# Trunk of retention, pooling, cross-attention and gated MLP: the value product's first weight splits are tied to the eleventh turned tile, and VectorE takes the pool groups' two carry copies from GpSimd

## The chip, the cores and the metric

The kernel runs on one core of one Trainium2 chip. The metric is device time in microseconds (us) of one launch, as the median of several runs. Beside the timed runs there is one profiled execution, whose trace gives start, length and waits of each instruction. All positions below are us from the start of that execution's span.

## The reference

One layer over a sequence of 2048 tokens with 1024 channels, all in f32. What matters here is the first half: a projection whose columns go to two mixers, an output projection with a residual, and a cross-attention into 256 memory tokens; a gated MLP and a last norm follow.

```
h = rmsnorm(x, mix_norm_g)
q, k, v, g, u = split(h @ w_in)
y_ret  = silu(g) * head_rmsnorm(retention(q, k, v))
# four channel groups of u, trailing windows 2, 4, 8, 16:
y_pool = ((window_sum(u) / count - u) @ pool_w) * pool_scale
x = x + concat(y_ret, y_pool) @ w_out
x = x + softmax(q' k'^T / 16) v' @ wo        # cross-attention, 4 heads
x = x + (silu(gate(c)) * val(c)) @ w_down    # c: causal conv of x_n @ w_up
out = rmsnorm(x, final_norm_g)
```

A trailing window of 16 tokens reaches back over the edge of a tile of tokens, so the kernel carries the last 16 columns of each group from one tile to the next.

## The kernel before, in words

Activations stand transposed: 128 channels on the partitions, tokens along the free dimension. The sequence is cut in two batches of 1024 tokens (`b` = 0, 1), each in two halves of 512 (`s`). Every f32 product is made of three TensorE passes (`passes`, L239): each operand is held as a rounded part and a rest, and high x high, high x low and low x high are added up in PSUM. So each weight tile and each activation tile that enters a product is first split: ScalarE writes the rounded part (L233, or L236 with a scale), and VectorE subtracts it from the source to get the rest (L234, which the profile books on the helper line L216, or L225 for the scaled form).

`unit` (L285) is one weight tile's work: `pairs` (L255) splits the tile's two halves into places of the tile Q, of which there are three; then 48 passes run, and an evacuation function is called per half of the tokens. `load_tile` (L303) fetches the tile into one of five places of R.

The stages of the first half, per batch: the value projection, four heads with their retention interleaved, the four pool groups in the order 0, 3, 2, 1 (in the second batch groups 3 and 2 come first of all, before the projection), the output projection (eight units whose contraction takes the groups' outputs last), the attention, and the value product (eight units, L1565 to L1580).

A pool group's evacuation (`pool_group`, L624) writes a half's 512 columns to a tile `u`, with 16 columns of room ahead of them. L630 copies the 16 carried columns `phalo` in there, L631 saves the last 16 columns of this half to `phalo` for the next. Then VectorE builds the window sum by doubling (additions over 527, 525, 521 and 513 columns, L636), takes the mean minus the token, and the result is split into the tile G. Both copies stand on GpSimd (the profile's POOL), in one queue with the DMAs that add up weight sums for the MLP (L915 to L922, four of them per job, each of which waits for an earlier one to land). POOL works its queue in order, as all engines do.

The attention (`attention`, L822) makes 16 score tiles (2 head pairs x 8 blocks of 128 tokens). For each: 24 passes, a row maximum on VectorE (L871), two exponentials on ScalarE (L875), the reciprocal (L877) and two scalings on VectorE, and `turn` (L847): four TensorE transposes (L850) and a split of the result. A tile is turned two tiles after its scores. The first tile needs the norm's factors, a chain of some 15 small VectorE operations (L267 to L272). In the second batch the MLP's first input tiles are normed beside it (`first_tiles`, L1453), on VectorE, GpSimd and the DMAs. The value product of the turned tiles follows; the last write of its weights VWd to DRAM is issued at 286.8 us, so for their fetch and split only room in R and Q and the engines' queues count.

The order of the instructions on each engine is set when the program is built, by a scheduler that plays the program through with its own durations; it places an instruction where its inputs are ready in that play. On the chip each engine then keeps that order.

Of the kernel before, what the change touches and what calls it, by code (L numbers as in the profile page):

```python
# [2 lines left out]

# [5 lines left out]
F32 = mybir.dt.float32  # L9
# [110 lines left out]
def trunk(ctx, tc, xT, memT, pos, w_qkgu, w_v, wkv, wqT, wo, wout_r, wout_p, poolT, w_up, w_dn, vecs, consts, outT):  # L120
# [94 lines left out]
    def tt(eng, out, a, b, op):  # L215
        return eng.tensor_tensor(out=out, in0=a, in1=b, op=op)  # L216
# [13 lines left out]
    def split(src, hi, lo, g=None):  # L230

        if g is None:
            act.activation(hi, src, AF.Copy)  # L233
            tt(dve, lo, src, hi.bitcast(F32), ALU.subtract)  # L234
        else:
            act.activation(hi, src, AF.Identity, scale=g)  # L236
            stt(lo, src, g, hi.bitcast(F32), ALU.mult, ALU.subtract)
# [17 lines left out]
    def pairs(raw):  # L255

        out = []
        for h in range(2):
            r = raw[h] if isinstance(raw, list) else raw[:, h * SUB : (h + 1) * SUB]
            pr = new_pair()  # L260
            split(r, pr[:, 0], pr[:, 1])
            out.append(pr)
        return out
# [13 lines left out]

    quarter, slow = [0], [True]
    behind, under, fetched = [iter(())], [iter(())], [None]

    def finish():
        for _ in behind[0]:
# [2 lines left out]
    def unit(raw, rhs, evac, order=range(4)):  # L285


        hs = pairs(raw)
        ps = [mmps() for _ in range(NS)]
        for h in range(2):  # L290
            for s in range(NS):
                for j, kk in enumerate(order):
                    k = 4 * h + kk
                    w = [hs[h][:, i, kk * P : (kk + 1) * P] for i in range(2)]
                    passes(ps[s], w, rhs(k, s), h + j == 0, h == 1 and j == 3)
                next(behind[0], None)
                quarter[0] += 1
                if not slow[0] or quarter[0] % 2:
                    next(under[0], None)
                if h == 1:  # L300
                    evac(s, ps[s])

    def load_tile(src, room=None):  # L303
        raw = new_raw() if room is None else room.f
        fetched[0] = sp.dma_start(raw, src.rearrange("p k n -> p (k n)"))
        return raw
# [317 lines left out]
    def pool_group(b, g, rb):  # L624
        out = B.take(2)

        def evac(s, ps):
            u, *bufs = [TT.take() for _ in range(3 if g else 2)]
            tt(dve, u.f[:, 16 : 16 + SUB], ps, rb[s].f[:, :SUB], ALU.mult)
            pool.tensor_copy(u.f[:, 0:16], phalo[:, g])  # L630
            pool.tensor_copy(phalo[:, g], u.f[:, SUB : SUB + 16])  # L631
            src, lo = u, 1
            for i in range(g + 1):
                sh = 1 << i
                dst = bufs[i % 2]
                tt(dve, dst.f[:, lo : 16 + SUB], src.f[:, lo : 16 + SUB], src.f[:, lo - sh : 16 + SUB - sh], ALU.add)  # L636
                src = dst
                lo += 2 * sh
            cur, d = u.f[:, 16 : 16 + SUB], src.f[:, 16 : 16 + SUB]
            w = 2 << g  # L640
            if b == 0 and s == 0:
                tt(dve, d[:, :w], d[:, :w], icnt[:, :w], ALU.mult)
                ts(dve, d[:, w:], d[:, w:], 1.0 / w, ALU.mult)
                tt(dve, d, d, cur, ALU.subtract)
            else:
                stt(d, d, 1.0 / w, cur, ALU.mult, ALU.subtract)
            split(d, out.r[:, s * SUB : (s + 1) * SUB], out.r[:, T + s * SUB : T + (s + 1) * SUB])
            for r in (u, *bufs):
                r.free()

        unit(load_tile(w_qkgu[12 + g]), xpair, evac)
        return out
# [152 lines left out]
    def add_residual(b, n, s_acc, got=None, acc=None):  # L805


        def evac(s, ps):
            cols = slice(s * SUB, (s + 1) * SUB)
            d = acc.f[:, cols] if got is None else got[s].f[:, :SUB]  # L810
            tt(dve, d, d, ps, ALU.add)
            if got is not None:
                split(d, *xpair(n, s))
                act.dma_start(Xd[b, n][:, cols], d)
            squares(n, d, s_acc[s].f[:, :SUB])
            if got is not None:
                got[s].free()

        return evac


    def attention(sums, beside, pace):  # L822


        scl, nscl = (smp.tile([P, 8], F32, tag="scl", name=nm("scl"), bufs=2) for _ in range(2))
        room = B.take(2 * KT)
        third = [Region(B, room.first + KT * i, KT) for i in range(2)] + [new_z(F32R).take(KT)]
        prob = [third[1], third[0]]

        def load_m(hp):  # L830

            out = mw[hp]
            for kp in range(KT // 2):
                raw = new_raw()
                fetched[0] = sp.dma_start(raw.rearrange("p (k n) -> p k n", k=2), Md[hp, 2 * kp : 2 * kp + 2].rearrange("k p n -> p k n"))
                if hp == 0 and kp == 0:

                    out += [(pr[:, 0], pr[:, 1]) for pr in pairs(raw)]
                    yield
                    continue  # L840
                for i in range(2):
                    u = third[2 * hp].r[:, (2 * kp + i) * T : (2 * kp + i + 1) * T]
                    split(raw[:, i * SUB : (i + 1) * SUB], u[:, :SUB], u[:, SUB:])
                    out.append((u[:, :SUB], u[:, SUB:]))
                yield

        def turn(pt, t, e):  # L847
            tp = aux()
            for j in range(4):
                pe.transpose(tp[:, j * P : (j + 1) * P], e.f[:, j * P : (j + 1) * P], ident)  # L850
            pt4 = pt.r.rearrange("p (i k t) -> p i k t", i=2, t=T)[:, :, :, t * P : (t + 1) * P]
            split(tp.rearrange("p (k t) -> p k t", k=4), pt4[:, 0], pt4[:, 1])
            e.free()

        mw = [[], []]
        for _ in load_m(0):
            pass
        more_m = load_m(1)
        late = []
        for i in range(2 * KT):  # L860
            hp, t = divmod(i, KT)
            ps = mmps()
            for k in range(KT):
                x2 = [X[:, 2 * k + j, t * P : (t + 1) * P] for j in range(2)]
                passes(ps, x2, mw[hp][k], k == 0, k == KT - 1)
            if i == 0:
                rn, _, _ = norm_tables(sums, wide=False)
                ts(dve, scl, rn, 1.0 / 16.0, ALU.mult)
                ts(dve, nscl, rn, -1.0 / 16.0, ALU.mult)
            mx, sm = small(2), small(2)  # L870
            dve.reduce_max(out=mx, in_=ps.rearrange("p (h m) -> p h m", h=2), axis=AX.X)  # L871
            ts(dve, mx, mx, nscl[:, t : t + 1], ALU.mult)
            e = TT.take()
            for j in range(2):
                act.activation(e.f[:, j * NMEM : (j + 1) * NMEM], ps[:, j * NMEM : (j + 1) * NMEM], AF.Exp,  # L875
                               bias=mx[:, j : j + 1], scale=scl[:, t : t + 1], accum_out=sm[:, j : j + 1])
            dve.reciprocal(sm, sm)  # L877
            for j in range(2):
                ej = e.f[:, j * NMEM : (j + 1) * NMEM]
                ts(dve, ej, ej, sm[:, j : j + 1], ALU.mult)  # L880
            if len(late) == 2:
                turn(*late.pop(0))
            late.append((prob[hp], t, e))
            for _ in range(pace):
                next(under[0], None)
            if i < KT - 2:
                next(more_m, None)
            else:
                for _ in range(pace):
                    next(beside, None)  # L890

        def end():
            for one in late:
                yield turn(*one)

        return prob, end()
# [599 lines left out]
    for b in range(NB):  # L1496
# [68 lines left out]
        for n in range(KT):  # L1565
            if n + 1 < KT:
                fetch_acc(n + 1)

            def rhs(k, s):
                at = (k % 4) * T + s * SUB  # L1570
                return tuple(prob[k // 4].r[:, i * 4 * T + at : i * 4 * T + at + SUB] for i in range(2))

            unit(load_tile(VWd[n]), rhs, add_residual(b, n, xs, acc=acc[n]))
            act.dma_start(Xd[b, n], acc[n].f)
            if b + 1 < NB:
                load_x(n, nxt, got)
                if n + 1 < KT:
                    got = fetch_x(b + 1, n + 1)
            elif n in (1, 3, 5):
                combine(rds[0], n // 2)  # L1580
# [143 lines left out]
```

## Time and profile before

| what | us |
|---|---|
| timed, three runs | 2504.08, 2498.81, 2500.07; median 2500.07 |
| profiled execution, its own time | 2497.77 |
| its span, first to last instruction | 2496.0 |
| TensorE busy (11390 passes) | 2439.3 (98%) |
| VectorE busy | 1699.9 (68%) |
| ScalarE busy | 1220.0 (49%) |
| GpSimd busy | 387.9 (16%) |

The profiled execution is 2.30 us below the median of the three runs. TensorE is busy nearly all the time, so the table alone shows that a change to the other engines can only act through the few stretches in which TensorE waits. In a timeline row, the number in brackets is how long the engine sat idle before the instruction, and the name behind the arrow is what ended that.

### The profile page before, as it was taken

How to read it: one execution, taken by the hardware profiler on the slowest of the kernel's cores; microseconds unless marked ns; L12 is line 12 of the kernel's file. 1: busy time of each engine (PE TensorE's matmuls, PEld its weight loads, DVE VectorE, ACT ScalarE, POOL GpSimd, SP SyncE). 2: the span in 40 equal slices, each digit the busy share in tenths (PEclk: the TensorE clock that was granted, in tenths of full speed). 3: DMA queues.
4: the chain of work that ended last, by engine and by line, in shares of the span. 5: the costliest groups of instructions: out<-in, count | busy, mean ns of one | idle time of the engine just before them, and what ended most of it. 6: DMA issues, size and time to landing. Idle time of an engine off the chain costs nothing. (4 is left out here: it accounts for less than half of the span.)

```text
span 2496.0 us, 33121 instructions
## 1 busy us (share of the span) xinstructions
PE 2439.3 (98%) x11390; PEld 2035.1 (82%) x11390; DVE 1699.9 (68%) x2757; ACT 1220.0 (49%) x2171; POOL 387.9 (16%) x396
## 2 busy tenths in 40 slices
PE   6999999999999999999998999999999999999997
PEld 6888887888788888888886888888888887888885
DVE  8646566564636574665777776896677687877875
ACT  6333423443321223424654555675555576666663
POOL 1010122100121110030025130332113021000001
PEclk9999999999999999999999999999999999999998
DMA  9363888716766664365567565665456468768951
GB/s 319 90 169 110 249 189 233 234 41 207 218 142 151 155 158 153 108 226 210 174 205 251 179 195 161 202 228 171 158 164 210 136 217 297 245 190 281 343 165 68
DMA packets 257176, 474.27 MB, mean 190 GB/s; under 512 B 26864, under 2 KB 56176, under 8 KB 257008
## 3 DMA queue, kind: packets, MB, share of 16 engines
q1 hardware_dynamic: 212336, 408.18, 48.9%
q0 software_dynamic: 19584, 34.61, 9.0%
q10 hardware_dynamic: 25088, 29.37, 3.4%
q8 instruction: 89, 1.46, 0.2%
q14 instruction: 79, 0.65, 0.1%
HBM read 370.87 MB, written 170.39 MB: 217 GB/s over the span
## 5 line engine op out<-in xcount | busy, mean ns | idle before, releaser
L241 PE MATMUL mm<-G,Q 128*128 128x512 f32 (+1 forms) x1888 | 727.7, 386 | 18.9 <-ACT Q L233 10.9
L243 PE MATMUL mm<-G,Q 128*128 128x512 f32 (+1 forms) x1888 | 725.3, 385 | 4.6 <-DVE Q L216 4.5
L242 PE MATMUL mm<-G,Q 128*128 128x512 f32 (+1 forms) x1888 | 725.1, 384 | 0.0
L241 PE MATMUL mm<-G 128*128 128x512 f32 (+1 forms) x1380 | 530.0, 386 | 7.4 <-DVE Z L216 7.4
L243 PE MATMUL mm<-G 128*128 128x512 f32 (+1 forms) x1380 | 530.9, 385 | 2.3 <-DVE G L216 2.3
L242 PE MATMUL mm<-G 128*128 128x512 f32 (+1 forms) x1380 | 531.4, 385 | 0.0
L241 PEld LDWEIGHTS mm<-G,Q 128*128 128x128 f32 x1888 | 357.7, 190 | 88.1 <-ACT Q L233 11.5
L243 PEld LDWEIGHTS mm<-G,Q 128*128 128x128 f32 x1888 | 357.2, 189 | 74.4 <-DVE Q L216 5.9
L242 PEld LDWEIGHTS mm<-G,Q 128*128 128x128 f32 x1888 | 357.7, 189 | 68.4 <-DVE G L216 0.4
L241 PEld LDWEIGHTS mm<-G 128*128 128x128 f32 x1380 | 259.8, 188 | 61.0 <-DVE Z L216 7.3
L243 PEld LDWEIGHTS mm<-G 128*128 128x128 f32 x1380 | 259.8, 188 | 54.3 <-DVE G L216 2.8
L242 PEld LDWEIGHTS mm<-G 128*128 128x128 f32 x1380 | 259.9, 188 | 51.5
L225 DVE SCALAR_TENSOR_TENSOR Z<-Z,vecs 128x1024 f32<-128x1024 f32 x176 | 244.7, 1393 | 55.8 <-ACT Z L1067 50.2
L1004 ACT ACTIVATE G<-R 128x512 fp32r<-128x512 f32 (+1 forms) x272 | 167.1, 616 | 230.0 <-PE mm L242 223.7
L216 DVE TENSOR_TENSOR G<-R,G 128x512 fp32r<-128x512 f32 (+1 forms) x268 | 196.7, 741 | 115.4 <-ACT G L1004 76.8
L216 DVE TENSOR_TENSOR Q<-R,Q 128x512 fp32r<-128x512 f32 x235 | 174.0, 742 | 148.1 <-ACT Q L233 138.4
L216 DVE TENSOR_TENSOR Z<-Z,mm 128x512 f32<-128x512 f32 x284 | 193.3, 681 | 88.3 <-PE mm L243 87.8
L233 ACT ACTIVATE Q<-R 128x512 fp32r<-128x512 f32 x150 | 93.9, 627 | 238.5 <-PE mm L242 194.0
L216 DVE TENSOR_TENSOR G<-T,G 128x512 fp32r<-128x512 f32 (+1 forms) x201 | 134.8, 685 | 51.1 <-ACT G L953 37.7
L1004 ACT ACTIVATE Q<-R 128x512 fp32r<-128x512 f32 (+1 forms) x204 | 125.3, 614 | 76.4 <-PE mm L242 60.5
L1067 ACT ACTIVATE Z<-Z,vecs 128x1024 f32<-128x1024 f32 x88 | 109.3, 1242 | 51.6 <-DVE Z L216 50.0
L216 DVE TENSOR_TENSOR T<-T 128x512 f32<-128x512 f32 (+4 forms) x161 | 109.6, 689 | 35.1 <-POOL T L630 17.6
(217 smaller groups left out, 2654.9 us busy)
## 6 DMA issues: line engine op xcount, KB each, us to landing
R<-Ud SPq DMA_DIRECT2D x176, 256.0 KB, 2.7
T<-Gd SPq DMA_DIRECT2D x168, 256.0 KB, 4.3
R<-w_up SPq DMA_DIRECT2D x132, 256.0 KB, 3.0
Gd<-Z SPq DMA_DIRECT2D x110, 256.0 KB, 2.5
Ud<-w_up SPq DMA_DIRECT2D x88, 256.0 KB, 5.9
R<-w_qkgu SPq DMA_DIRECT2D x32, 512.0 KB, 4.3
R<-Dd SPq DMA_DIRECT2D x64, 256.0 KB, 4.1
Gd<-T SPq DMA_DIRECT2D x56, 256.0 KB, 3.1
```

The lines of the kernel that those rows point to most:

```text
L216: return eng.tensor_tensor(out=out, in0=a, in1=b, op=op)
L225: dve.scalar_tensor_tensor(out=out, in0=a, scalar=s, in1=b, op0=op0, op1=op1)
L233: act.activation(hi, src, AF.Copy)
L241: pe.matmul(ps, lh, rh, start=start, stop=False, skip_group_check=more)
L242: pe.matmul(ps, lh, rl, start=False, stop=False, skip_group_check=more)
L243: pe.matmul(ps, ll, rh, start=False, stop=stop, skip_group_check=more)
L1004: act.activation(p2[:, 0, :w], self.raw[i].f[:, :w], AF.Copy)
L1067: act.activation(self.c[g].f, a[:, 2:], AF.Identity, bias=cb[:, f : f + 1], scale=cw[2][:, f : f + 1])
```

## The change

Three things are edited. The two carry copies of a pool group's evacuation go from GpSimd to VectorE. The turned tiles' split is written out so that the ScalarE instruction of each is kept in a list. And for the first two units of the value product the weights are fetched and split ahead of `unit`, under a mark that makes their ScalarE instructions stand behind the split of the eleventh turned tile (index 10) in ScalarE's queue; the VectorE subtractions follow by their data.

```
     def unit(raw, rhs, evac, order=range(4)):
-        hs = pairs(raw)
+        hs = raw if isinstance(raw, list) else pairs(raw)
...
             tt(dve, u.f[:, 16 : 16 + SUB], ps, rb[s].f[:, :SUB], ALU.mult)
-            pool.tensor_copy(u.f[:, 0:16], phalo[:, g])
-            pool.tensor_copy(phalo[:, g], u.f[:, SUB : SUB + 16])
+            dve.tensor_copy(u.f[:, 0:16], phalo[:, g])
+            dve.tensor_copy(phalo[:, g], u.f[:, SUB : SUB + 16])
...
-            split(tp.rearrange("p (k t) -> p k t", k=4), pt4[:, 0], pt4[:, 1])
+            turned.append(act.activation(pt4[:, 0], tp.rearrange("p (k t) -> p k t", k=4), AF.Copy))
+            tt(dve, pt4[:, 1], tp.rearrange("p (k t) -> p k t", k=4), pt4[:, 0].bitcast(F32), ALU.subtract)
...
-            unit(load_tile(VWd[n]), rhs, add_residual(b, n, xs, acc=acc[n]))
+            with tc.issue_after(turned[10].ins) if n < 2 else nullcontext():
+                weights = pairs(load_tile(VWd[n]))
+            unit(weights, rhs, add_residual(b, n, xs, acc=acc[n]))
```

There are 16 evacuations of pool groups (4 groups x 2 halves x 2 batches), so 32 copies move. The edit adds five lines to the file: the copies L630 and L631 of before are L631 and L632 now, L871 is L874, L877 is L880. Behind the second batch's attention no engine's order is changed.

The first place is VectorE in the first batch's pool group 2 (mm_2972 and mm_2973 are the PSUM tiles of its first and second half, T the temporaries, among them those of group 3's second half, Q the split weights). Lines with + are new or moved there:

```order
 L216 TENSOR_TENSOR T<-mm_2973,T 128x512
 L216 TENSOR_TENSOR Q<-R,Q 128x512
+L631 COPY T<-phalo 128x16
 L225 SCALAR_TENSOR_TENSOR T<-aux_2925,vecs,T 128x512
 L216 TENSOR_TENSOR T<-mm_2972,T 128x512
+L632 COPY phalo<-T 128x16
 L216 TENSOR_TENSOR T<-T 128x527
 L216 TENSOR_TENSOR G<-T,G 128x512
+L631 COPY T<-phalo 128x16
+L216 TENSOR_TENSOR T<-T 128x525 x2
+L632 COPY phalo<-T 128x16
 L216 TENSOR_TENSOR T<-T 128x527
```

Between the evacuation of mm_2972 and the additions over 527 columns now stands one copy of VectorE's own, where before the additions needed a copy out of this piece of GpSimd's queue:

```order
L915 DMA Ud<-w_up 128x512
L916 DMA Ud<-w_up 128x512
L919 DMA Ud<-Ud 128x512
L630 COPY T<-phalo 128x16
L631 COPY phalo<-T 128x16
L630 COPY T<-phalo 128x16
```

Of these only the DMAs are left on GpSimd.

The second place is VectorE at the start of the first batch's attention, in the norm's chain (sm_3788, sm_3789 and sm_3791 hold its values, mm_3753 is the first score tile). Before:

```order
L871 TENSOR_REDUCE sm_3805<-mm_3753 128x2
L225 SCALAR_TENSOR_TENSOR sm_3791<-sm_3791,sm_3788 128x8
L216 TENSOR_TENSOR Q<-R,Q 128x512
L225 SCALAR_TENSOR_TENSOR sm_3789<-sm_3791,sm_3789 128x8
L216 TENSOR_TENSOR sm_3791<-sm_3789 128x8
```

And now:

```order
L874 TENSOR_REDUCE sm_3805<-mm_3753 128x2
L225 SCALAR_TENSOR_TENSOR sm_3791<-sm_3791,sm_3788 128x8
L225 SCALAR_TENSOR_TENSOR sm_3789<-sm_3791,sm_3789 128x8
L216 TENSOR_TENSOR sm_3791<-sm_3789 128x8
L225 SCALAR_TENSOR_TENSOR sm_3791<-sm_3791,sm_3788 128x8
```

The rest of a value-product weight (Q<-R,Q) has left the chain; so has its rounding on ScalarE, which stood ahead of the first exponential.

The third place is VectorE in the second batch's attention, at the eleventh turned tile (aux_8232); mm_8198 is the thirteenth score tile and sm_8224 its row sums.

```order
L874 TENSOR_REDUCE sm_8223<-mm_8198 128x2
L220 TENSOR_SCALAR sm_8223<-sm_8223,scl_7593 128x2
L216 TENSOR_TENSOR G<-aux_8232,G 128x4x128
L216 TENSOR_TENSOR Q<-R,Q 128x512 x3
L880 RECIPROCAL sm_8224<-sm_8224 128x2
L220 TENSOR_SCALAR T<-T,sm_8224 128x256 x2
```

Three rests of the value product's weights now stand together ahead of that tile's reciprocal; before, they stood some five tiles earlier, one at a time. In the first batch three stand together in the same way. Two further copies of L631 (group 3 and group 2 of the second batch, which start while the norm of that batch is made) now stand in VectorE's stretch of that norm, the later one between `rn` (L1415) and the cast behind it (L328).

More of the change, by code (lines that the diff above doesn't have):

```diff
@@ L1 @@
 import math
-from contextlib import ExitStack
+from contextlib import ExitStack, nullcontext
 import concourse.bass as bass
@@ L279, in trunk @@
     behind, under, fetched = [iter(())], [iter(())], [None]
+    turned = []
     def finish():
@@ L851, in turn @@
             pt4 = pt.r.rearrange("p (i k t) -> p i k t", i=2, t=T)[:, :, :, t * P : (t + 1) * P]
-            split(tp.rearrange("p (k t) -> p k t", k=4), pt4[:, 0], pt4[:, 1])
+            turned.append(act.activation(pt4[:, 0], tp.rearrange("p (k t) -> p k t", k=4), AF.Copy))
+            tt(dve, pt4[:, 1], tp.rearrange("p (k t) -> p k t", k=4), pt4[:, 0].bitcast(F32), ALU.subtract)
             e.free()
+        turned.clear()
         mw = [[], []]
```

## The prediction

> **What bounds the kernel now.** First the shares of the engines and TensorE's clock on the page, then TensorE's own waits, then the places of those waits in the timeline.
>
> ```profile
> PE 2439.3 (98%) x11390; PEld 2035.1 (82%) x11390; DVE 1699.9 (68%) x2757; ACT 1220.0 (49%) x2171; POOL 387.9 (16%) x396
> PEclk9999999999999999999999999999999999999998
> ```
>
> TensorE is busy for 2439.3 of 2496.0 us at nine tenths or more of its full clock in all but the last slice. What other engines can give or take lies in the 56.7 us that are left, and those are few, single waits. TensorE's list of waits names them (engine and line that waited, who ended it, us in total, times, longest):
>
> ```profile
> PE mm L241 <- ACT G L233: 3.0, 2, 2.1
> PE aux L339 <- DVE G L216: 1.8, 1, 1.8
> PE aux L850 <- DVE T L220: 1.6, 3, 0.9
> PE aux L315 <- DVE T L216: 0.7, 1, 0.7
> ```
>
> These four lines are all of TensorE's waits near the edited code, 7.1 us. The rest of its idle time lies at the start, at the end and in the MLP, where no instruction changes its place. So the change cannot win more than 7.1 us, 0.28%, and to lose as much it would have to make new waits. Now each in the timeline.
>
> **The copies, first batch.** TensorE, ScalarE, VectorE and GpSimd around the 2.1 us wait:
>
> ```profile
> 390.28 0.80 PE L241 MATMUL mm<-G,Q 128*128 128x512 f32 x1 [2.11 <-ACT G L233]
> ...
> 389.59 1.23 ACT L233 ACTIVATE G<-T 128x512 fp32r<-128x512 f32 x2 [7.04 <-DVE T L216]
> ...
> 374.09 0.68 DVE L216 TENSOR_TENSOR T<-mm,T 128x512 f32<-128x512 f32 x1
> 382.79 0.71 DVE L216 TENSOR_TENSOR T<-T 128x527 f32<-128x527 f32 x1 [8.02 <-POOL T L630]
> ...
> 381.74 0.81 POOL L919 DMA_DIRECT2D Ud<-Ud  x1 [4.59 <-DMA Ud<-w_up]
> 382.27 0.48 POOL L630 COPY T<-phalo 128x16 f32<-128x16 f32 x1
> ```
>
> Read from the top, this is one chain. TensorE waits from 388.17 to 390.28 for group 2's rounded output; ScalarE rounds it at 389.59, behind VectorE; VectorE lay idle for 8.02 us up to 382.79, for one copy of 16 columns on GpSimd; and that copy stood behind L919, a weight-sum DMA that waited 4.59 us for another DMA to land. With the copy on VectorE, none of this queue is in the chain. By the new order three copies stand between mm_2972's evacuation and the rounded output. A copy of this size on VectorE does not occur before; the nearest are 8 columns wide:
>
> ```profile
> 673.64 0.17 DVE L1412 COPY rn<-sm 128x8 f32<-128x8 f32 x1
> 673.85 0.17 DVE L327 CAST yh<-rn 128x8 fp32r<-128x8 f32 x1
> 674.06 1.29 DVE L216 TENSOR_TENSOR G<-consts,yh 128x512 fp32r<-128x512 f32 x2
> 674.89 0.47 PE L339 MATMUL aux<-G,ones 128*128 128x512 f32 x1 [1.85 <-DVE G L216]
> ...
> 662.29 0.38 PE L315 MATMUL aux<-consts,T 128*128 128x1 f32 x2 [0.70 <-DVE T L216]
> ```
>
> They start 0.21 us apart. Three copies are 0.6 us, so the output comes 8.02 - 0.6 = 7.4 us earlier, at 382.2, and TensorE asks for it at 388.17. **-2.11 us**, with 6 us to spare; what is late next is group 1, whose evacuation stands behind this on VectorE and comes forward with it. The bounds: the whole wait goes (-2.11), or another input of the same stretch holds it (0).
>
> **The copies, second batch.** The other wait of that line:
>
> ```profile
> 933.22 0.50 PE L241 MATMUL mm<-G,Q 128*128 128x512 f32 x1 [0.86 <-ACT G L233]
> ...
> 931.69 0.75 DVE L225 SCALAR_TENSOR_TENSOR T<-aux,vecs,T 128x512 f32<-128x512 f32 x1 [0.79 <-PE aux L777]
> ```
>
> It stands behind a retention head, whose transposes (L777), product and rounding the change leaves alone: 0. But two copies now stand on VectorE in the stretch that makes this batch's norm, and there TensorE does wait, by the last two rows of the fence before 1.85 and 0.70 us, on VectorE itself. Each copy lengthens one of them by 0.17 to 0.21: **+0.4 us**. The bounds are 0, if the first one's delay is taken up in a wait for a weight load, and 1.0, two copies at the 487 ns median that GpSimd needs for one:
>
> ```profile
> L630 POOL COPY T<-phalo x16: 196/487/1285, 333.8 to 920.7; 128x16 f32<-128x16 f32 x16
> ```
>
> I take 0.4, by the row on VectorE itself. The other copies (27 of 32) lie where VectorE idles or where TensorE does not wait for it; 27 x 0.2 = 5.4 us of VectorE's 796 idle ones.
>
> **The splits at the start of the first attention.** ScalarE, VectorE and TensorE there:
>
> ```profile
> 480.84 0.61 ACT L355 ACTIVATE T<-T 128x512 f32<-128x512 f32 x1
> 489.13 0.63 ACT L233 ACTIVATE Q<-R 128x512 fp32r<-128x512 f32 x1 [7.68 <-DMA R<-VWd]
> 492.62 1.28 ACT L875 ACT_TABLE_LOAD   x1 [2.85 <-DVE sm L220]
> ...
> 485.20 0.16 DVE L225 SCALAR_TENSOR_TENSOR sm<-sm,sm 128x8 f32<-128x8 f32 x1
> 489.80 0.69 DVE L216 TENSOR_TENSOR Q<-R,Q 128x512 fp32r<-128x512 f32 x1 [4.44 <-ACT Q L233]
> 490.41 0.16 DVE L225 SCALAR_TENSOR_TENSOR sm<-sm,sm 128x8 f32<-128x8 f32 x1
> ...
> 495.35 0.62 DVE L220 TENSOR_SCALAR T<-T,sm 128x256 f32<-128x256 f32 x2
> ...
> 495.76 0.70 PE L850 MATMUL aux<-consts,T 128*128 128x128 f32 x4 [0.87 <-DVE T L220]
> ```
>
> A weight that is needed only when the tiles are turned was placed in the norm's chain; its load landed late, ScalarE waited for it, VectorE behind ScalarE, and the norm's chain lay still from 485.36 to 490.41, 5.05 us. Without it the scaled tile comes at 495.97 - 5.05 = 490.9, and TensorE wants it at 495.76 - 0.87 = 494.89: **-0.87 us**, with 4 us of cover. Bounds: -0.87 and 0.
>
> **The splits at the eleventh turned tile.** What was spread is now one block of three per batch. In the first batch VectorE idles some 3 us per tile there (the first row below), so it costs nothing. In the second (the other rows) it is the tight place, since the MLP's first tiles are normed beside it:
>
> ```profile
> 551.78 0.69 DVE L871 TENSOR_REDUCE sm<-mm 128x2 f32<-128x512 f32 x1 [2.90 <-PE mm L243]
> ...
> 1094.42 0.68 DVE L216 TENSOR_TENSOR G<-aux,G 128x512 fp32r<-128x512 f32 x1
> 1095.92 0.17 DVE L877 RECIPROCAL sm<-sm 128x2 f32<-128x2 f32 x1 [0.82 <-ACT T L875]
> 1096.18 2.07 DVE L220 TENSOR_SCALAR T<-T,sm 128x256 f32<-128x256 f32 x2
> 1099.53 0.75 DVE L225 SCALAR_TENSOR_TENSOR T<-T,vecs 128x512 f32<-128x512 f32 x1 [1.28 <-DMA T<-Xd]
> ...
> 1100.15 0.60 PE L850 MATMUL aux<-consts,T 128*128 128x128 f32 x4
> ...
> 1109.89 0.44 PE L850 MATMUL aux<-consts,T 128*128 128x128 f32 x2 [0.21 <-DVE T L220]
> ...
> 1114.09 0.41 PE L850 MATMUL aux<-consts,T 128*128 128x128 f32 x2 [0.57 <-DVE T L220]
> ...
> 1106.44 0.48 PE L241 MATMUL mm<-G,Q 128*128 128x512 f32 x1
> ...
> 1095.43 2.67 POOL L216 TENSOR_TENSOR T<-T 128x512 f32<-128x512 f32 x2 [0.94 <-DMA Hd<-T]
> ```
>
> The block of three goes between the rows at 1094.42 and 1095.92. Three subtractions at the median of the next quoted row, 0.685, are 2.06 us, of which 0.82 fill an idle gap: the reciprocal, the scaling and the tile come 1.24 us later, ready at 1099.49 instead of 1098.25 (1096.18 + 2.07), and TensorE turns that tile at 1100.15. So 0.66 us are left, and the 1.28 us of idling behind it end the delay. **0**. The weights are ready by about 1098, and their first product is at 1106.44. Bounds: below, -0.78, the last two tiles' waits (0.21 and 0.57), since the old subtractions stood where the MLP's tiles begin and these may now run earlier; above, the longest subtraction of this form:
>
> ```profile
> L216 DVE TENSOR_TENSOR Q<-R,Q x235: 674/685/1785, 10.5 to 2439.1; 128x512 fp32r<-128x512 f32 x118
> ```
>
> Three at 1.785 are 5.36 us; less 0.82 idle and 1.90 of slack (1100.15 - 1098.25), TensorE waits 2.6.
>
> **The sum**, against the profiled execution's 2497.77: -2.11 + 0.4 - 0.87 + 0 = -2.58, which gives 2495.2. That execution is 2.30 us below the median of the three runs, and it is their median that is to be met: 2500.07 - 2.58 = **2497.5 us**, 0.10% less.
>
> **The rivals.**
> *One wait stays.* Another input of the same chain holds it, above all in the pool groups, where a split weight stands between the additions. Against it: the ScalarE half of that split ran long before, and 6 us are to spare. It gives 2498.3 to 2499.6.
> *The tail goes too.* The MLP's first tiles start earlier, and VectorE is free at 1109 and 1114: 0.78 us more, and the norm's copies cost nothing: 2496.3. For it speaks that three subtractions leave the stretch in which those tiles begin; against it that their later steps hang on loads (the 1.28 <-DMA above).
> *Slower: the block meets GpSimd.* The row of GpSimd shows it adding tiles from 1095.43 to 1098.10, just where the block falls, and the scaling beside it took 2.07 where 0.62 is usual (the row at 495.35). If each of the three waits for a GpSimd addition (2.67 / 2 = 1.34 us each), they take 3 x (0.69 + 1.34) = 6.1 us; less 0.82 and 1.90 TensorE loses 3.4 us, which outweighs the 2.6 won: 2500.9. It decides from 2.6 us of loss on, that is from 5.3 us for the three.
> [...]
> That the change does not do what it says is small: by the order of the instructions both stalls' releasers have left their chains.
>
> **How the numbers follow.** Forecast 0.60, one wait stays 0.13, the tail goes 0.15, slower 0.12. The three runs before lie 1.3 below to 4.0 above their median, so each case has a scatter of 2 to 3 us. From 2496.3 less some 3 to 2500.9 plus some 1.5 the range is 2493 to 2502.5. A measurement of this kernel can tell about 0.2% (5 us) from no change. More than that is won where the forecast (1 in 5) or the tail (1 in 2) meets a good scatter: 0.12 + 0.08 + 0.01 = 0.21. It is lost in half of the slow case and rarely else: 0.06 + 0.02 = 0.08. Within 0.2%: 0.71.
>
> **What would show it.** In the profile after, VectorE's 8.02 us wait for a copy and TensorE's 2.11 us wait near 390 are gone; the norm chain at 485 runs through, and TensorE turns its first tile without waiting; TensorE's waits near 660 and 675 are 0.1 to 0.3 longer each; the block of three stands near 1092, each about 0.7 us, with no wait of TensorE at 1100 or at the value product's start. Wrong would be a new wait of TensorE in the pool groups, a VectorE copy that waits for its buffer, or subtractions of over 1.5 us in the block. TensorE's busy time should stay within 1 us.

## The result and the profile after

The changed kernel takes 2495.22 us, the median of 12 runs (2493.16 to 2497.89), against 2500.68 us for the kernel before (12 runs, 2497.06 to 2508.43). The ratio is 0.9976, 95% interval 0.9967 to 0.9985: 6 us less, with an interval from 3.8 to 8.3 (the medians differ by 5.5 us). The prediction was 2497.5 us and -2.6 us (0.10%). The time lies in its range and moved the way that was forecast, but by about twice as much, and -0.24% lies just outside the "within 0.2%" that was held likeliest. Two later groups of runs of the same two kernels gave 0.9981 each (intervals 0.9972 to 0.9991 and 0.9972 to 0.9990), just inside it.

First the page's line on the engines, then TensorE's list of waits (engine and line that waited, who ended it, us in total, times, longest):

```profile
PE 2441.3 (98%) x11390; PEld 2039.3 (82%) x11390; DVE 1704.0 (68%) x2789; ACT 1220.2 (49%) x2171; POOL 374.2 (15%) x364
```

```profile
PE mm L241 <- ACT T L491: 2.3, 1, 2.3
PE aux L340 <- DVE G L216: 1.5, 1, 1.5
PE aux L316 <- DVE T L216: 1.0, 1, 1.0
...
PE mm L241 <- ACT G L233: 0.9, 1, 0.9
```

The 32 copies have left GpSimd (396 instructions before, 364 now) and cost VectorE 4 us. Of the four lines shown of before, the one on the turned tiles (L850 then, L851 now) is gone, with all its three waits, and the pool group's 2.1 is gone from L241's line; the 0.9 that is left there is the retention head's. A new 2.3 on L491 stands near 277, in code that the change does not touch. That profiled execution, 2497.84 us, is one of the slowest two of the 12, so the span alone (2495.7 against 2496.0) would have shown no gain at all.

The pool group, in the timeline of the changed kernel:

```profile
378.37 0.60 PE L778 MATMUL aux<-consts,T 128*128 128x128 f32 x4
...
379.68 0.68 DVE L216 TENSOR_TENSOR T<-mm,T 128x512 f32<-128x512 f32 x1
...
380.39 0.17 DVE L632 COPY phalo<-T 128x16 f32<-128x16 f32 x1
380.48 0.70 DVE L216 TENSOR_TENSOR T<-T 128x527 f32<-128x527 f32 x1
...
381.47 0.81 POOL L925 DMA_DIRECT2D Ud<-Ud  x1 [7.16 <-DMA Ud<-Ud]
...
387.82 1.14 ACT L233 ACTIVATE G<-T 128x512 fp32r<-128x512 f32 x2
```

VectorE goes from the evacuation (379.68) to the additions (380.48) without the 8.02 us of idling, though GpSimd's queue waits for its DMA now as it did then (7.16 us at 381.47).

The norm's chain at the first attention:

```profile
486.61 0.36 DVE L225 SCALAR_TENSOR_TENSOR sm<-sm,sm 128x8 f32<-128x8 f32 x2
...
488.22 0.17 DVE L1415 COPY rn<-sm 128x8 f32<-128x8 f32 x1
...
491.76 0.62 DVE L220 TENSOR_SCALAR T<-T,sm 128x256 f32<-128x256 f32 x2
...
495.70 0.60 PE L851 MATMUL aux<-consts,T 128*128 128x128 f32 x4
```

It runs through. The first scaled tile is ready at 492.38 and TensorE turns it at 495.70 without waiting, 3.3 us later.

### The profile page after: what moved, and what is told of

The parts are those of the page before. It is cut to its first block, busy times and chain, and to the rows that moved or that the text cites. A ratio compares the mean times of both kernels' runs of the same rounds, so it can differ in the third digit from the quotient of the medians.

```text
span 2495.7 us, 33069 instructions
## 1 busy us (share of the span) xinstructions
PE 2441.3 (98%) x11390; PEld 2039.3 (82%) x11390; DVE 1704.0 (68%) x2789; ACT 1220.2 (49%) x2171; POOL 374.2 (15%) x364
## 3 DMA queue, kind: packets, MB, share of 16 engines
q8 instruction: 89, 1.46, 0.2%
## 5 line engine op out<-in xcount | busy, mean ns | idle before, releaser
L241 PE MATMUL mm<-G,Q 128*128 128x512 f32 (+1 forms) x1888 | 728.3, 386 | 16.1 <-ACT Q L233 10.5
L241 PE MATMUL mm<-G 128*128 128x512 f32 (+1 forms) x1380 | 531.5, 387 | 10.4 <-DVE Z L216 7.3
L241 PEld LDWEIGHTS mm<-G,Q 128*128 128x128 f32 x1888 | 358.2, 190 | 84.2 <-ACT Q L233 11.2
L241 PEld LDWEIGHTS mm<-G 128*128 128x128 f32 x1380 | 260.4, 189 | 64.6 <-DVE Z L216 6.3
L941 ACT ACTIVATE aux<-R 128x512 f32<-128x512 f32 (+1 forms) x184 | 105.4, 575 | 47.8 <-DVE Q L216 23.8
```

What stands on the lines that cost most here:

```text
L241: pe.matmul(ps, lh, rh, start=start, stop=False, skip_group_check=more)
L941: act.activation(t, x, AF.Copy)
```

## The experiments

Thirteen profiles were taken in all, with those two above. The diffs are against the changed kernel. Each ratio below is to the kernel before, on the same chip in the same group of runs; its median there was 2498.31, 2496.11 and 2500.95 us in the three groups (the first two on one chip, the third on another), so times of different groups, which move by as much as the change is worth, are not compared.

### The kernel before once more, and the changed one

No edit.

> The kernel before, unchanged, for a second profiled execution and for the scatter. All theories: a ratio of 1.000, interval about 0.001 to each side. Theory 'sizes vary' (the waits that the change removes end on loads, so they are longer in the usual execution than in the one that was profiled): TensorE's waits in the pool groups and at the first attention's start add up to something clearly other than 2.11 + 0.87 us, the likeliest 4 to 6 us. Theory 'trace sum' (the waits of the first profile are typical, and the measured -0.24% is the -3.8 us of the traces plus scatter): the same two places, 2.1 and 0.9 us to within some 0.3.

Measured: 0.9998 (0.9987 to 1.0009). In this profile of the same program the two places look otherwise. TensorE waits 1.10 and 0.68 us in the pool groups, and at the first attention 2.37 us. There TensorE, ScalarE and VectorE read:

```profile
489.79 0.15 DVE L225 SCALAR_TENSOR_TENSOR sm<-sm,sm 128x8 f32<-128x8 f32 x1
495.20 0.63 ACT L233 ACTIVATE Q<-R 128x512 fp32r<-128x512 f32 x1 [8.68 <-DMA R<-VWd]
495.87 0.69 DVE L216 TENSOR_TENSOR Q<-R,Q 128x512 fp32r<-128x512 f32 x1 [5.92 <-ACT Q L233]
496.48 0.16 DVE L225 SCALAR_TENSOR_TENSOR sm<-sm,sm 128x8 f32<-128x8 f32 x1
...
501.83 1.11 PE L850 MATMUL aux<-consts,T 128*128 128x128 f32 x4 [2.37 <-DVE T L220]
502.60 0.78 PE L242 MATMUL mm<-G 128*128 128x512 f32 x1
503.17 0.63 PE L243 MATMUL mm<-G 128*128 128x512 f32 x1
503.60 0.63 PE L241 MATMUL mm<-G 128*128 128x512 f32 x1
...
505.26 0.39 PE L242 MATMUL mm<-G 128*128 128x512 f32 x1
505.49 0.40 PE L243 MATMUL mm<-G 128*128 128x512 f32 x1
```

The two places add up to 4.15 us instead of 2.98, which is for "sizes vary". The load came later, so the chain lay still for 6.69 us, from the start of one operation to the start of the next (489.79 to 496.48), instead of 5.21 (485.20 to 490.41; the 5.05 of the prediction count from the first one's end). And the passes behind the wait start 0.43 us apart (503.17, 503.60) where 0.23 is usual (505.26, 505.49). The windows of granted clock say the same. Each row gives a stretch and its length, then the busy time (and instructions) of TensorE, its weight loads, VectorE, ScalarE and GpSimd, then the granted clock, the DMA share and GB/s; first this place, then the first profile's pool group:

```profile
500.00:505.00 5.00, 3.17 (x10) 2.69 (x11) 2.28 (x9) 3.44 (x13) 0.81 (x1) 0.68 1.03 229
```

```profile
386.00:390.00 4.00, 2.17 (x10) 1.47 (x8) 4.00 (x9) 0.41 (x1) 1.84 (x3) 1.00 0.58 105
390.00:394.00 4.00, 3.72 (x10) 2.94 (x11) 4.00 (x8) 1.34 (x3) 1.46 (x3) 0.57 1.05 356
394.00:398.00 4.00, 4.00 (x19) 3.31 (x18) 3.91 (x7) 0.63 (x1) 2.22 (x5) 1.00 0.88 130
```

10 passes in the 3.72 busy us behind the 2.11 us wait, 19 in the next 4.00. So the cost of the wait in the prediction's largest term was not over when the wait was: TensorE then ran at half clock for 3.4 us. In the trace's record of the clock that stretch is 3.41 us long (390.20 to 393.61), at 0.50, and loses half of that, 1.7 us. The page's row of the clock, 62 us to a digit, had not shown it.

> The changed kernel, unchanged, for a second profiled execution. Both theories: no wait of TensorE near 390, 495, 1100 to 1114. Theory 'trace sum': ratio 0.9985 (-3.8 us: pool wait 2.11, first attention 0.87, last turned tiles 0.78). Theory 'sizes vary': ratio 0.9976 again, and 5.5 to 6 us. The 2.3 us wait near 277 that the first profile of it showed, in code that is the same in both kernels, should be gone or elsewhere, if it is scatter of a load.

Measured: 0.9981 (0.9972 to 0.9991); no wait near 390, 495 or 1100 to 1114, and a wait of 2.5 us on L491 near 277 again. So that wait belongs to both kernels (before had it in its second profile, 2.25 us); it comes and goes with the landing of a store (ScalarE's wait for `VWd<-T` there is 8.5 to 8.8 us in these three profiles and 3.9 in the first of before).

### Each half alone

```
-            with tc.issue_after(turned[10].ins) if n < 2 else nullcontext():
+            with tc.issue_after(turned[10].ins) if False else nullcontext():
```

> Only the 32 copies go to VectorE; the value product's first weights are split where they were. Trace sum: the 2.11 us near 390 go, the 0.87 us at 495 stay, the waits at 1109 and 1114 stay (0.8 together), the second batch's norm costs 0 to 0.4: -2.0 us, ratio 0.9992. Sizes vary: -2 to -5 us, and if the pool wait is the one that varies, ratio 0.998.

Measured: 0.9987 (0.9978 to 0.9996), 3.2 us. The wait near 390 is gone. The late load is still there, but it cost nothing this time:

```profile
483.70 0.16 DVE L225 SCALAR_TENSOR_TENSOR sm<-sm,sm 128x8 f32<-128x8 f32 x1
486.40 0.63 ACT L233 ACTIVATE Q<-R 128x512 fp32r<-128x512 f32 x1 [6.22 <-DMA R<-VWd]
487.07 0.69 DVE L216 TENSOR_TENSOR Q<-R,Q 128x512 fp32r<-128x512 f32 x1 [3.21 <-ACT Q L233]
487.68 0.16 DVE L225 SCALAR_TENSOR_TENSOR sm<-sm,sm 128x8 f32<-128x8 f32 x1
```

The chain lay still for 3.98 us. The three profiles with the splits in the chain agree with one another: 6.69, 5.21 and 3.98 us of standstill, 2.37, 0.87 and 0 of waiting. In the first two the difference is 4.3 us; that much the turn can bear.

```
-            dve.tensor_copy(u.f[:, 0:16], phalo[:, g])
-            dve.tensor_copy(phalo[:, g], u.f[:, SUB : SUB + 16])
+            pool.tensor_copy(u.f[:, 0:16], phalo[:, g])
+            pool.tensor_copy(phalo[:, g], u.f[:, SUB : SUB + 16])
```

> Only the weight splits are tied to the eleventh turned tile; the copies stay on GpSimd. Trace sum: the 0.87 us at 495 and the 0.78 us of the last turned tiles go, the pool group's wait near 390 stays: -1.65 us, ratio 0.9993. Sizes vary: -1.5 to -4 us; if the first attention's wait is the one that varies, ratio 0.9985. The rival of the block that meets GpSimd's additions: the three subtractions near 1094 take over 5.3 us and TensorE waits at 1100; in the first profile after they took 4.0 and it did not.

Measured: 0.9994 (0.9984 to 1.0004). TensorE's waits at the edited places:

```profile
PE mm L241 <- ACT G L233: 2.9, 2, 2.1
PE aux L851 <- DVE T L220: 2.6, 2, 1.9
...
PE mm L242 <- DVE G L216: 0.7, 1, 0.7
```

The pool group waits as before (2.09 and 0.70 us), this time without a half-clock stretch. The interval contains 1, so this half alone is not told from no change; but the two halves, 3.2 and 1.5 us, add up to the 4.7 of the changed kernel in the same group. The first turn and the last ones do not wait, but two turns inside the first attention do (0.79 from 509.56 on, 1.85 from 534.27 on). They stand behind other loads, VectorE 7.91 us behind the load of the positions and ScalarE 3.95 us behind one of xT. The other profiles have 0 to 1.43 us at the second of these places, so it is the next thing to be late there.

### What one wait costs

Each weight unit but the pool groups' got one wait, 56 in all: a product of one column, a chain of VectorE operations on it, a product of one column on the end of the chain, and all of TensorE's later work queued behind that. The wrapper that does this puts every TensorE instruction on its own line, L107.

```
+    def probe(last):
+        n = (2, 5, 8, 11, 14)[probes[0] % 5]
...
+        with tc.issue_after(last.ins):
+            pe.matmul(ps[:, :1], ident, one, start=True, stop=True)
+        ts(dve, v, ps[:, :1], 1.0, ALU.mult)
+        for _ in range(n):
+            ts(dve, v, v, 1.0, ALU.mult)
+        pe.gate = pe.matmul(ps[:, 1:2], ident, v, start=True, stop=True)
```

> The changed kernel with 56 waits of TensorE put into it on purpose, one in each weight unit but the pool groups': a tiny product, a chain of 3, 6, 9, 12 or 15 small VectorE operations on its result, a second tiny product on the end of the chain, and everything on TensorE queued behind that. The chains make the waits about 1.2, 1.8, 2.4, 3.0 and 3.6 us long, 11 of each. It measures what one wait costs. Theory 'length': a wait costs its length, and the clock granted after it stays at 1.00; the kernel is longer by the sum of the waits, some 135 us. Theory 'clock' (what a wait costs depends on whether it makes the clock gate close: then TensorE runs at half clock for 3.4 us and loses 1.7 us more): none or few of the 1.2 us waits are followed by a stretch at 0.50, about half of those of 2.0 to 2.5 us, all or nearly all of 3.4 us and more; 25 to 40 such stretches, and 45 to 70 us on top of the sum of the waits.

Measured: 2837.67 us in one run. The span is 2835.9 us, 340.2 more than in the changed kernel's first profile, and TensorE's busy time 2567.1 us, 125.8 more. The sum of the waits, and two of them with what follows (a wait of 1.11, a wait of 3.80):

```profile
PE aux L107 <- DVE sm L234: 199.6, 56, 11.8
```

```profile
801.03 0.38 PE L107 MATMUL aux<-sm,consts 128*128 128x1 f32 x2 [1.11 <-DVE sm L234]
801.28 3.02 PE L107 MATMUL mm<-G,Q 128*128 128x512 f32 x12
```

```profile
1077.78 0.38 PE L107 MATMUL aux<-sm,consts 128*128 128x1 f32 x2 [3.80 <-DVE sm L234]
1078.03 5.28 PE L107 MATMUL mm<-G,Q 128*128 128x512 f32 x15
```

12 passes in 3.02 us, but 15 in 5.28: at the first one's pace they would take 3.8. The waits came out longer than meant (199.6 us, not 135), since the chains stood behind VectorE's other work. TensorE's busy time inside half-clock stretches is 209 us, half of which, 104, is the clock's price, 96 more than in the changed kernel. Of the other 30 us of busy time the added products of one column are some 27: such products alone fill 39.6 us here and 12.7 in the changed kernel. Of all 13 profiles, the waits that stand alone (no other of over 0.5 us within 12 us):

| wait, us | number | followed by half clock |
|---|---|---|
| 0.8 to 1.4 | 49 | 2 (both in the second batch's norm) |
| 1.4 to 2.0 | 12 | 3 |
| 2.0 to 2.6 | 14 | 9 |
| 2.6 to 3.1 | 9 | 6 |
| 3.1 and more | 29 | 29 |

The low stretches are 3.41 us or a multiple of that, but for the last, which the end of the program cuts. "Length" falls: it allows 199.6 us of the 340.2. "Clock" stands, though its 25 to 40 stretches and 45 to 70 us were too few for waits that long: there are 79 units of 3.41 us.

At one place the same wait goes either way. Near 277, waits of 1.86, 2.23, 2.25 and 2.32 us halved the clock in four profiles and 2.48 us did not in a fifth. The traces show where the cases differ: within a profile all half-clock stretches start whole multiples of 3.413 us apart (80 of them from 390.2 to 663.3 in the first profile). On this grid, which lies elsewhere in each profile (a piece starts at 276.37 in one and at 274.88 in the other), the 2.32 us of the changed kernel's first profile fall into one piece, and the 2.48 us of its second are split between two:

```profile
276.37:279.79 3.42, 1.10 (x5) 0.59 (x4) 1.38 (x2) 1.19 (x3) 0.81 (x1) 1.00 0.09 19
279.79:283.20 3.41, 3.41 (x13) 2.92 (x12) 1.29 (x2) 2.52 (x5) 0.00 (x0) 0.50 1.06 184
```

```profile
274.88:278.29 3.41, 1.63 (x8) 1.01 (x6) 1.38 (x2) 0.04 (x1) 0.33 (x1) 1.00 0.17 55
278.29:281.70 3.41, 2.71 (x15) 2.35 (x16) 1.29 (x2) 2.52 (x4) 0.48 (x1) 1.00 0.65 74
```

The piece of the first is idle for 68% of its length and half clock follows; the two of the second are idle for 52% and 21%, and the clock stays. Take all pieces of the 13 profiles that ran at full clock, between 80 us and the last 40, and count as idle also the products of one column (16 of them stand close together in the second batch's norm, where half clock followed the shortest waits). None of 8936 that were idle for under 54% was followed by half clock, 4 of 8 between 54 and 56% were, and all 74 above that. This sorting was made on the same traces that it describes; no further run tested it. It fits the 2.09 us near 390 of the splits-only kernel too, whose piece is idle for 51%.

### Which engine copies

```
-            dve.tensor_copy(u.f[:, 0:16], phalo[:, g])
-            dve.tensor_copy(phalo[:, g], u.f[:, SUB : SUB + 16])
+            act.activation(u.f[:, 0:16], phalo[:, g], AF.Copy)
+            act.activation(phalo[:, g], u.f[:, SUB : SUB + 16], AF.Copy)
```

> As the changed kernel, but the 32 copies go to ScalarE instead of VectorE. Theory 'queue' (the wait near 390 came from the copy's place in GpSimd's queue behind the weight-sum DMAs, and any other engine cures it): no wait of TensorE near 390, ratio as the changed kernel's, 0.997 to 0.9985. Theory 'VectorE' (it matters that producer and consumer of the columns are one engine, since a ScalarE copy also waits in a queue, behind roundings that wait for loads): a wait of 1 us or more stays in the pool groups or comes in the second batch's norm, ratio 0.9985 to 1.000.

Measured: 0.9977 (0.9965 to 0.9990). TensorE's only wait on ScalarE's G<-T is the retention head's:

```profile
PE mm L241 <- ACT G L233: 0.9, 1, 0.9
```

With the copies on ScalarE the wait near 390 is gone as it is with them on VectorE. With the 8.02 us behind a copy that itself took 0.48, it is GpSimd's queue that made the wait.

> Copies on ScalarE, splits tied as in the changed kernel. The wait near 390 was gone with ScalarE too, so 'queue' expects the changed kernel's ratio to within 0.1%; if the copies cost something in VectorE's norm chain of the second batch (the 0.4 us of the prediction), 0.2 to 0.4 us less than the changed kernel, which no ratio here can show but TensorE's waits near 665 can: 1.3 to 1.6 us together against 1.3 to 2.5 with VectorE's copies.

Measured: 0.9976 (0.9965 to 0.9987), beside the changed kernel on the same chip:

> The changed kernel once more, beside the next two on one chip. Accounting 'waits and clock': the kernel before loses 3.8 to 5.2 us in waits at the edited places and 1.7 us more for each that closes the clock gate, 5.4 to 6.9 us by its two profiles; ratio 0.9972 to 0.998. 'Length' alone: 0.9985.

Measured: 0.9981 (0.9972 to 0.9990). The two are not told apart. Then the copies on VectorE in the first batch only:

```
-            dve.tensor_copy(u.f[:, 0:16], phalo[:, g])
-            dve.tensor_copy(phalo[:, g], u.f[:, SUB : SUB + 16])
+            (dve if b == 0 else pool).tensor_copy(u.f[:, 0:16], phalo[:, g])
+            (dve if b == 0 else pool).tensor_copy(phalo[:, g], u.f[:, SUB : SUB + 16])
```

> As the changed kernel, but in the second batch the copies stay on GpSimd; only the first batch's 16 go to VectorE. If the gain of the copies is all at the wait near 390, as the trace says: the changed kernel's ratio to within 0.1%, no wait near 390. If the second batch's copies on VectorE cost 0.4 us in the norm, TensorE's waits near 665 and 673 are that much shorter here, 1.0 to 2.1 together; if they cost nothing, 1.3 to 2.5 as in the changed kernel. If on the other hand the second batch has a wait behind GpSimd's queue too, a new wait of 0.5 us or more shows in its pool groups, near 680 to 700 or 890 to 925.

Measured: 0.9974 (0.9965 to 0.9983), no new wait in the second batch's pool groups. The gain of the copies lies in the first batch. TensorE's two waits in the second batch's norm together: 2.55, 2.12 and 2.56 us in the three profiles with all copies on GpSimd, 1.46 in this one, 2.53, 1.54, 1.68, 1.35, 1.57 and 2.07 with VectorE, 1.31 and 1.72 with ScalarE. The 1.46 fits both expectations, and nothing here shows that VectorE's copies lengthen the waits.

### Where the block stands

```
-            with tc.issue_after(turned[10].ins) if n < 2 else nullcontext():
+            with tc.issue_after(turned[7].ins) if n < 2 else nullcontext():
```

> As the changed kernel, but the splits stand behind the eighth turned tile instead of the eleventh. In the second batch the block then falls near 1075, between two stretches of GpSimd additions (1067.3 to 1072.7 and 1078.6 to 1084.3 in the profile after). If the block's 4.0 us came from meeting GpSimd, the subtractions take 0.65 us each there, 1.9 to 2.1 together, as in the first batch; if they are slow in that stretch for another reason (three writes in a row, loads), 3 us or more. Either way TensorE does not wait there, and the ratio is the changed kernel's, 0.997 to 0.9985.

Measured: 0.9986 (0.9975 to 0.9997). First the second batch's block of the changed kernel, on VectorE (the row, then the shortest, middle and longest of its three in ns) and GpSimd, then the same three subtractions here:

```profile
1093.55 4.01 DVE L216 TENSOR_TENSOR Q<-R,Q 128x512 fp32r<-128x512 f32 x3
...
L216 DVE TENSOR_TENSOR Q<-R,Q x3: 679/1702/1777, 1093.5 to 1096.9; 128x512 fp32r<-128x512 f32 x3
...
1093.40 3.00 POOL L216 TENSOR_TENSOR T<-T 128x512 f32<-128x512 f32 x2 [0.40 <-DMA Hd<-T]
```

```profile
1071.68 1.28 DVE L216 TENSOR_TENSOR Q<-R,Q 128x512 fp32r<-128x512 f32 x2
1072.89 0.74 DVE L225 SCALAR_TENSOR_TENSOR T<-T,vecs 128x512 f32<-128x512 f32 x1
1073.55 0.68 DVE L216 TENSOR_TENSOR Q<-R,Q 128x512 fp32r<-128x512 f32 x1
...
1065.76 5.39 POOL L216 TENSOR_TENSOR T<-T 128x512 f32<-128x512 f32 x4 [135.83 <-ACT T L878]
1076.99 3.00 POOL L216 TENSOR_TENSOR T<-T 128x512 f32<-128x512 f32 x2 [5.84 <-DVE T L225]
```

With GpSimd idle (1071.15 to 1076.99) a subtraction takes 0.68 us; beside its two additions three take 4.01, and 3.98 to 4.01 in all seven profiles with the block there. The first two take 1.70 and 1.78 us, and the third, which starts at 1096.87 when GpSimd has been done since 1096.40, takes 0.68 again. TensorE waits in neither kernel.

```
-            with tc.issue_after(turned[10].ins) if n < 2 else nullcontext():
+            with tc.issue_after(turned[13].ins) if n < 2 else nullcontext():
```

> As the changed kernel, but the splits stand behind the fourteenth turned tile: how much room the place has on its late side. The fourteenth tile's rounding was at 570.3 and 1107.0 in the profile after, about when TensorE begins the value product; three roundings and the first subtraction behind it take some 2.6 us. Both theories of the clock expect a wait of TensorE of 2 to 4 us at each of the two value products; 'length' gives +0 to +3 us against the kernel before (the changed kernel's -5 and twice 2 to 4), 'clock' up to 3.4 us more: ratio 1.000 to 1.003.

Measured: 0.9998 (0.9984 to 1.0011). TensorE at the second value product:

```profile
1106.41 0.50 PE L241 MATMUL mm<-G,Q 128*128 128x512 f32 x1 [0.34 <-ACT Q L233]
...
1108.75 0.50 PE L243 MATMUL mm<-G,Q 128*128 128x512 f32 x1 [1.14 <-DVE Q L216]
```

The waits are 0.77 us in the first batch and 1.69 in the second (0.21, 0.34 and 1.14), less than the 2 to 4 expected, and half clock follows none of them. By the trace three tiles later is too late, by 2.5 us of waits; the ratios do not show it, since the intervals of the eighth, the eleventh (with the copies on ScalarE in this group) and the fourteenth tile overlap.

## Why the prediction was right or wrong

The accounting, for the edited places (us of TensorE's waiting, and half-clock stretches behind it):

| profile | pool groups near 390 | first turn | last turns | stretches |
|---|---|---|---|---|
| before | 2.11 | 0.87 | 0.78 | 1 |
| before, again | 1.79 | 2.37 | 1.04 | 1 |
| changed, three profiles | 0 | 0 | 0 | 0 |
| copies only | 0 | 0 | 0.18 | 0 |
| splits only | 2.79 | 0 | 0 | 0 |
| tie to the eighth tile | 0 | 0 | 0 | 0 |
| copies on ScalarE, two | 0 | 0 | 0, 0.41 | 0 |
| copies moved in the first batch only | 0 | 0 | 0.53 | 0 |

With 1.7 for a stretch, before loses 5.5 and 6.9 us there, and the changed kernel nothing. That stands against 6.0, 4.7 and 4.8 us from the three ratios. The ratios do not decide between this and the waits alone, 3.8 and 5.2, since their intervals hold both; that the stretch is real is shown by its passes, and that such stretches cost time, by the added waits.

- **The copies, first batch: right place, price too small.** The rounded output was to come 7.4 us earlier; from the same transposes of the retention on (L777 before, L778 now) it came after 16.81 us before (372.78 to 389.59) and after 9.45 now (378.37 to 387.82), 7.36 less. But -2.11 took the wait's length for its price. With the clock it was 3.8 in that execution; in the next 1.8, in the splits-only kernel 2.8.
- **The copies, second batch: +0.4 was too much, 0 to 0.2 is left.** For the later copy the rows show why. It stands in a gap that the norm's chain has anyway, between a result and its use:

```profile
673.93 0.17 DVE L1415 COPY rn<-sm 128x8 f32<-128x8 f32 x1
674.01 0.17 DVE L631 COPY T<-phalo 128x16 f32<-128x16 f32 x1
674.13 0.17 DVE L328 CAST yh<-rn 128x8 fp32r<-128x8 f32 x1
```

  The cast starts 0.20 us behind `rn`, as it did without the copy (0.21). The 0.21 that the prediction took for an instruction's length is in this chain the time from an operation to one that needs its result; the copy, which needs none of the chain, started 0.08 behind `rn`. The first copy, at 658.70, stands in a run of VectorE without a gap up to the operation that ends TensorE's wait at 667.43, and may cost the 0.2 there. That is not shown: the wait was 0.98 us against 0.70 in the two first profiles, but 0.50 to 0.97 with the copies on GpSimd and 1.26 or less with them on VectorE, and the second wait, near 675, was 1.55 against 1.85.
- **The first attention: the mechanism was right, the size not a constant.** 4 us of cover were predicted and 4.3 found; what differs is how late the load lands. The wait is 0, 0.87 or 2.37 us, the last with a half-clock stretch: 0 to 4.1 us, not 0.87.
- **The block, 0: right for TensorE, wrong for the block.** It was to show subtractions of 0.7 us, and over 1.5 was named as a sign of being wrong: two of the three take 1.70 and 1.78. They were slow beside GpSimd's additions, as the slower rival supposed. It priced 6.1 us for three and found 2.7 of cover and the point of decision at 5.3: measured were 4.0, below it. There were two additions to meet, not three. Three subtractions of 0.65 (1.28 for two, above) and two additions of 1.35 (5.39 for four, above) one after the other would be 4.65 us, and from 1093.40 to 1097.56 it took 4.2: the two engines' work ran nearly one after the other.
- **The tail goes too: the rival came true.** The last turns' 0.78 was put at a bound and at 15%. It is 0 in the three profiles of the changed kernel, against 0.78 and 1.04 of before. But two variants with the same tie have 0.41 and 0.53, and the copies-only kernel, without the tie, 0.18, so the tie is not shown to be the whole of it.
- **"TensorE's busy time should stay within 1 us": wrong.** It is 2435.9 to 2442.9 us in the 12 profiles without added waits, 2439.3 and 2442.9 for the same program. Less half of what lies in half-clock stretches (between 80 us and the last 40) it is 2432.6 to 2435.5. So "what other engines can give or take lies in the 56.7 us" of idle time was wrong too, and the bound of 7.1 us rests on it: waits also set how fast TensorE runs while it is busy. (The list of waits has 1.1 us on L749 at 229.62 and 0.4 on L777 besides, in the retention, not at the start, at the end or in the MLP; neither changed the sum.)

The step that failed is the price of a wait: the sum made it its length, and one execution's length at that. With the 1.7 us of the half-clock stretch, the tail's 0.78 and the 0.2 to 0.4 of the copies that did not come, the first profile's -2.6 becomes -5.3 to -5.5. That the sum on the profiled execution, 2495.2 us, is the measured median is luck: the terms were too small by 2.7 to 2.9 us, and that execution lay 2.9 us below the median of the 12 runs before. None of the variants beats the changed kernel beyond the intervals; the best, copies in the first batch only and copies on ScalarE, are at 0.9974 to 0.9977.

## What to carry to other kernels

Where TensorE is the bound, price a wait of 2 to 3 us as its length plus a good chance (15 of 23 here) of 1.7 us more, and look at the granted clock in windows of a few us around it, not in the page's forty slices. A wait that hangs on a load can have another size in each execution (0, 0.87 and 2.37 us at the first attention here), so take a second profile before the price of its removal is trusted. Keep small copies that gate a bound engine out of a queue that waits for DMAs (8.02 us of VectorE's idling hung on one of 0.48 us here); which other engine takes them mattered little here (0.9976 and 0.9977 with ScalarE, 0.9976 to 0.9981 with VectorE).

## What was not expected of the hardware

A wait of TensorE of 2.0 to 3.1 us halved its clock in 15 of 23 cases, and all 29 longer ones did; the low stretches came in units of 3.41 us on a grid of that step. Of the grid's pieces at full clock, all 74 that were idle for over 56% were followed by half clock, and none of 8936 idle for under 54%, where products of one column count as idle. Three VectorE subtractions (Q<-R,Q) took 4.01 us beside two GpSimd additions in the second batch, and 1.89 us in the first (553.75), where GpSimd was idle.
